# Rows for the FFN turned by the DMA engines as two 16-bit halves, and a new order of steps, in the SSD phase of a hybrid decoder layer

## The chip, the cores and the metric

One NeuronCore of a Trainium2 chip runs the whole layer in one launch. Times are device microseconds of that core. The engines are named as in the profile: PE (TensorE, matrix products and its weight loads PEld), DVE (VectorE), ACT (ScalarE), POOL (GpSimd), and SP (SyncE), whose queue issues nearly all DMAs.

## The reference

A decoder layer on 2048 tokens of 1024 columns, in float32. What matters here is how its two sub-layers meet: the first mixes tokens (an SSD half and an RWKV-7 half, 512 columns each) and projects the result; the second is a gated FFN that reads normalised rows.

```python
mix = jnp.concatenate([y_ssd, y_rwkv], axis=-1).astype(h.dtype) @ w_out[l]
h = h + _rms_norm(mix, post_mix_norm[l])
hn = _rms_norm(h, pre_ffn_norm[l])
u = _causal_dwconv(hn @ ffn_w_up[l], ffn_conv_w[l], ffn_conv_b[l])
...
def _rms_norm(x, g):
    xf = x.astype(jnp.float32)
    y = xf * lax.rsqrt(jnp.mean(xf * xf, axis=-1, keepdims=True) + NORM_EPS)
```

The FFN multiplies `hn` from the left, so PE needs it with the 1024 columns on the partitions: rows have to be turned into columns on the way. This is the place of the change.

## The kernel before

Three phases follow each other and overlap at their ends. Phase R (to about 1000 us) makes the projections and the RWKV half. Phase S (about 1000 to 1440 us) does the SSD half, the output projection and both norms. Phase F is the FFN. Large products are made in float16 with each operand split into a high and a low half. Phase R turns its own input rows by DMA transposes of such halves (lines 399 and 400, 128 rows by 1024 columns each).

Phase S works on sixteen chunks of 128 tokens. Its loop runs steps n = 1 to 15, each written out by the table `S_PLAN`: a word `c.x` calls method `x` of chunk n, `n.` of chunk n+1, `p.` of n-1, `q.` of n-2, and `s.`/`t.` of a pair of chunks in even or odd steps. `Z` is one of four parts of a later chunk's gate product `z` (three per step, four from step 13 on). PE executes in exactly this order. The other engines' and SP's orders are set by a scheduler that simulates times. After the loop, the table `S_TAIL` mixes the last methods with `F`, pieces of phase F's beginning.

The methods: `begin` turns the inputs (`px`) and makes the scores (`psc`); `decay` makes `Dt`, from the rows R of the running sums (`bc` on PE, exponentials on ACT); `off` adds the old state's part (`pf`); `y` multiplies (`py`); `norm` turns the result (`pY`) and splits it into `Y`; `state` updates the state (`pst`); `keys` turns the keys (`pb`); `o` projects in parts (`yr` is the RWKV half, `xi` loads the residual rows). The pair's methods `steps` (`dt`), `sums` and `flip` (`acs`) make the running sums, which go to DRAM (`rows`) and come back as R for each chunk (`n.rows`).

`post`, in two parts, is the end of a chunk: Square of `m` on ACT with a sum over the row (its elementwise output is junk, written into `hT`), reciprocal root on POOL (`pov`, `por`), gain on DVE, residual added on POOL, write of H, a second Square, `pnv` and `pnr`, and the normalised row on DVE, written over `xi`. Then part 0 and part 1 each turn four blocks of 128 columns on PE (tile `ht`), ACT copies them to `hT`, and after part 1 one DMA writes HN, from which phase F reads its operands `hs`.

```python
ps = (bank(f"ht{self.cf}{part}", "yb") if n >= N - 2 else bank(f"ht{self.cf}{part}", "o", 2))
for u in range(4):
    kt = 4 * part + u
    nc.tensor.transpose(ps[:, u, :], self.xin[:, kt * P:(kt + 1) * P], K.ident)
S.activation(self.hT[:, 4 * part:4 * part + 4, :], ps, AF.Copy)
```

Of the kernel before, what the change touches and what calls it, by code (L numbers as in the profile page):

```python
# [7 lines left out]
F32 = mybir.dt.float32  # L8
F16 = mybir.dt.float16
BF16 = mybir.dt.bfloat16  # L10
AF = mybir.ActivationFunctionType
ALU = mybir.AluOpType
# [5 lines left out]
D = 1024  # L18
P = 128
KT = 8  # L20
# [126 lines left out]
class Space:  # L147
# [27 lines left out]
    "Dt", "pp rr ones3 E", "identb mnegb", "Btok", "Xdt", "Xd", "aend dec sgs sgv sgr", "ST0 ST1", "sq", "yt0",  # L175
)
S_RIGHT = (
    "ident_s mhalf_s", "ssm pov por ss pnv pnr", "Y", "yr", "xi", "m", "gpost", "gpre2", "hT", "yt", "wo",
)
F_EARLY = ("us", "s3", "b0", "b1", "b2", "b3")  # L180
F_MID = (
# [8 lines left out]
c.decay.1 m.z.2 m.z.3 t.steps u.z.0 u.z.1 u.z.2 n.rows c.y u.z.3 c.state  # L190
"""
S_PLAN = """
c.begin c.decay.0 Z c.off p.norm c.keys Z c.decay.1 p.o.0.0 Z t.sums s.steps p.o.0.1 t.flip Z n.rows q.post.0 c.y c.state
p.o.1.0 q.post.1 p.o.1.1
"""
S_QUOTA = (3,) * 12 + (4,) * 3
S_TAIL = """
F F p.o.0.0 p.norm F p.o.0.1 p.o.1.0 p.o.1.1 F q.post.0 F q.post.1 F F F F F F p.post.0 F p.post.1
"""
FIRST = """  # L200
w.0 w.1 w.2 w.3 f.d.0 w.4 w.5 l. f.d.1 f.d.2 f.low.0 f.d.3 w.6 f.low.1 f.d.4 f.d.5 w.7 w.8 f.keys f.scan w.9 w.10 f.norm f.d.6 w.11 f.d.7 f.d.8 f.d.9 f.receptance w.12 f.gram.0 w.13 w.14 w.15 w.16 f.gram.1 f.solve.1 w.17 f.d.10 f.conv.0 w.18 w.19 n.load f.chain.0 f.chain.1 f.conv.1 f.chain.2 w.20 f.d.11 f.d.12 f.d.13 w.21 f.conv.2 f.transposed.0 f.conv.3 f.conv.4 f.conv.5 f.transposed.1 f.conv.6 f.chain.3 f.conv.7
# [42 lines left out]
def bcast_row(tc, K, pool, i, name):  # L244
    t = pool.tile([P, D], F32, name=name)
    tc.nc.scalar.dma_start(t, K.rows[i].partition_broadcast(P))
    return t
# [14 lines left out]
def rsqrt_cols(tc, K, pool, ss, n, scale, eps, name, psum=False, bufs=1):  # L262

    nc = tc.nc
    v = pool.tile([P, n], F32, name=name + "v", tag=name + "v", bufs=bufs)
    r = pool.tile([P, n], F32, name=name + "r", tag=name + "r", bufs=bufs)
    (nc.vector if psum else nc.gpsimd).tensor_scalar(out=v, in0=ss, scalar1=scale, scalar2=eps, op0=ALU.mult, op1=ALU.add)  # L267
    nc.gpsimd.tensor_tensor(out=r, in0=v, in1=K.mhalf[:, :n], op=ALU.pow)  # L268
    return r
# [518 lines left out]
def phase_S(tc, K, x, w_z, w_dt, w_o, XN, XC, YR, H, HN, blocks=8):  # L788
    nc = tc.nc
    V, S, G_ = nc.vector, nc.scalar, nc.gpsimd  # L790
    TB = 256
    wk, psp = Space(tc, "s_"), Space(tc, "sp_", space=PSUM)
# [50 lines left out]
    def bank(name, tag, bufs=1):  # L843
        return psp.tile([P, 4, P], F32, name=name, tag=tag, bufs=bufs)
# [81 lines left out]
    class Chunk:  # L926
# [146 lines left out]
        def post(self, part):  # L1073

            m, n = self.m, self.n
            if part == 0:
                ss = wk.tile([P, 1], F32, name="ssm" + self.cf, tag="ssm")
                self.hT = wk.tile([P, KT, P], F32, name="hT" + self.cf, tag="hT")
                jk = self.hT.rearrange("p a b -> p (a b)")[:, 0:D // 2].bitcast(BF16)
                S.activation(jk, m, AF.Square, accum_out=ss)  # L1080
                r = rsqrt_cols(tc, K, wk, ss, 1, 1.0 / D, EPS, "po")
                V.scalar_tensor_tensor(out=m, in0=m, scalar=r[:, 0:1], in1=gpost, op0=ALU.mult, op1=ALU.mult)
                G_.tensor_tensor(out=m, in0=m, in1=self.xin, op=ALU.add)
                K.marks[n] = nc.sync.dma_start(H[n], m)
                ss = wk.tile([P, 1], F32, name="ssh" + self.cf, tag="ss")
                S.activation(jk, m, AF.Square, accum_out=ss)
                r = rsqrt_cols(tc, K, wk, ss, 1, 1.0 / D, EPS, "pn")
                V.scalar_tensor_tensor(
                    out=self.xin, in0=m, scalar=r[:, 0:1], in1=gpre2, op0=ALU.mult, op1=ALU.mult)
            ps = (bank(f"ht{self.cf}{part}", "yb") if n >= N - 2 else bank(f"ht{self.cf}{part}", "o", 2))  # L1090
            for u in range(4):
                kt = 4 * part + u
                nc.tensor.transpose(ps[:, u, :], self.xin[:, kt * P:(kt + 1) * P], K.ident)
            S.activation(self.hT[:, 4 * part:4 * part + 4, :], ps, AF.Copy)
            if part == 1:
                nc.sync.dma_start(HN[n // 8][:, :, P * (n % 8):P * (n % 8) + P], self.hT)


    N = 2 * blocks
# [45 lines left out]
    gpost = bcast_row(tc, K, wk, 1, "gpost")  # L1145
    gpre2 = bcast_row(tc, K, wk, 2, "gpre2")
# [759 lines left out]
```

## Time and profile before

| | |
|---|---|
| median of three runs | 2689.52 us (2687.17 to 2689.76) |
| the profiled execution | 2683.97 us, its span 2681.7 us |
| busy share of PE, DVE, ACT, POOL | 92%, 71%, 45%, 46% |
| mean granted clock of PE | 0.971 |
| bytes moved by DMA | 310.74 MB, 116 GB/s over the span |

The span is the time from the first to the last instruction of the profiled execution. Busy shares are means over all phases; what a stage is worth is read from its own windows. A row of a group gives the summed time, the mean of one instruction in ns, and the idle time of the engine just before, with what ended it.

### The profile page before, as it was taken

How to read it: one execution, taken by the hardware profiler on the slowest of the kernel's cores; microseconds unless marked ns; L12 is line 12 of the kernel's file. 1: busy time of each engine (PE TensorE's matmuls, PEld its weight loads, DVE VectorE, ACT ScalarE, POOL GpSimd, SP SyncE). 2: the span in 40 equal slices, each digit the busy share in tenths (PEclk: the TensorE clock that was granted, in tenths of full speed). 3: DMA queues.
4: the chain of work that ended last, by engine and by line, in shares of the span. 5: the costliest groups of instructions: out<-in, count | busy, mean ns of one | idle time of the engine just before them, and what ended most of it. 6: DMA issues, size and time to landing. Idle time of an engine off the chain costs nothing. (4 is left out here: it accounts for less than half of the span.)

```text
span 2681.7 us, 53948 instructions
## 1 busy us (share of the span) xinstructions
PE 2475.0 (92%) x21340; PEld 1556.0 (58%) x21340; DVE 1909.1 (71%) x3655; ACT 1207.9 (45%) x2467; POOL 1223.6 (46%) x1324
## 2 busy tenths in 40 slices
PE   5889999999999889999997899999999999999998
PEld 4788888888888855555543344444443444444443
DVE  6768777777777665567677868787789836465557
ACT  6445555555565453344444543434354333123132
POOL 2344444444545343234467565656657523222135
PEclk8899999999999989999999999999999999999999
DMA  6323232232223252334455434443435543333252
GB/s 212 73 61 73 53 60 57 65 81 53 57 60 73 89 174 98 107 115 143 128 194 171 156 138 157 134 169 122 159 124 188 183 149 100 103 102 102 87 158 106
DMA packets 309341, 310.74 MB, mean 116 GB/s; under 512 B 168160, under 2 KB 213600, under 8 KB 305760
## 3 DMA queue, kind: packets, MB, share of 16 engines
q1 hardware_dynamic: 307792, 305.72, 37.9%
q8 instruction: 167, 2.74, 0.4%
q10 hardware_dynamic: 1296, 1.58, 0.2%
q14 instruction: 86, 0.70, 0.1%
HBM read 187.85 MB, written 110.99 MB: 111 GB/s over the span
## 5 line engine op out<-in xcount | busy, mean ns | idle before, releaser
L1378 PE MATMUL u<-b,w 128*128 128x512 f16 x3696 | 816.6, 383 | 30.4 <-ACT w L1219 16.1
L1378 PEld LDWEIGHTS <-w 128*128 128x128 f16 x3696 | 363.3, 99 | 480.0 <-issue 29.7
L289 PE MATMUL d<-xt,wr 128*128 128x129 f16 x5376 | 336.9, 224 | 18.1 <-DMA xt<-xh 15.3
L1614 PE MATMUL d<-dw,fa 128*128 128x512 f16 x1512 | 336.4, 381 | 10.6 <-DVE dw L1578 8.4
L289 PEld LDWEIGHTS <-wr 128*128 128x128 f16 x5376 | 322.8, 100 | 32.5 <-ACT wr L252 15.2
L1614 PEld LDWEIGHTS <-fa 128*128 128x128 f16 x1596 | 157.2, 98 | 212.9 <-issue 26.9
L1396 DVE TENSOR_TENSOR C<-u,C 128x512 f32<-128x512 f32 x220 | 150.5, 685 | 163.0 <-PE u L1378 162.6
L289 PE MATMUL c<-xt,wc 128*128 128x131 f16 x3072 | 205.3, 227 | 23.3 <-ACT tr L429 10.4
L289 PEld LDWEIGHTS <-wc 128*128 128x128 f16 x3072 | 189.4, 100 | 39.9 <-issue 31.9
L1627 DVE TENSOR_TENSOR acc<-d,acc 128x512 f32<-128x512 f32 x212 | 140.2, 682 | 51.8 <-PE d L1614 51.2
L576 DVE TENSOR_TENSOR tmp<-atl,xl 128x60 f32<-128x60 f32 (+24 forms) x465 | 139.5, 300 | 44.9 <-DMA atl<-ATd 28.7
L1431 DVE SCALAR_TENSOR_TENSOR p<-C,fpar,p 128x1024 f32<-128x1024 f32 x88 | 126.4, 1437 | 57.0 <-ACT p L1427 53.6
L1224 POOL TENSOR_TENSOR fa<-p,fa 128x512 f16<-128x512 f32 x100 | 133.2, 1350 | 70.8 <-ACT fa L1219 70.8
L1226 DVE SCALAR_TENSOR_TENSOR w<-us,w 128x512 f16<-128x512 f32 x132 | 116.5, 889 | 61.2 <-ACT w L1219 60.2
L452 DVE SCALAR_TENSOR_TENSOR ca<-rc,cw,ca 128x128 f32<-128x128 f32 x384 | 132.3, 389 | 22.8 <-POOL ca L447 22.6
L1219 ACT ACTIVATE fa<-p 128x512 f16<-128x512 f32 x110 | 66.5, 626 | 162.6 <-DVE p L1444 138.8
L579 DVE TENSOR_TENSOR xl<-xl,tmp 128x60 f32<-128x60 f32 (+24 forms) x465 | 124.7, 268 | 11.3
L1437 POOL COPY fcarry<-C 128x2 f32<-128x2 f32 x88 | 36.1, 410 | 182.6 <-DVE C L1396 182.2
L1431 DVE SCALAR_TENSOR_TENSOR a<-C,fpar,a 128x1024 f32<-128x1024 f32 x88 | 114.3, 1299 | 6.4 <-ACT a L1427 4.6
L1219 ACT ACTIVATE w<-us 128x512 f16<-128x512 f32 x132 | 80.0, 622 | 81.0 <-POOL us L1350 61.9
L1392 ACT ACTIVATE C<-u 128x512 f32<-128x512 f32 x88 | 51.8, 589 | 142.7 <-PE u L1378 125.7
L689 POOL TENSOR_TENSOR tS<-S,Pi 64x256 f32<-64x256 f32 x64 | 40.4, 632 | 163.5 <-DVE S L699 161.1
(316 smaller groups left out, 4550.3 us busy)
## 6 DMA issues: line engine op xcount, KB each, us to landing
UW<-w SPq DMA_DIRECT2D x154, 256.0 KB
w<-UW SPq DMA_DIRECT2D x154, 256.0 KB
us<-in_w_u_dram SPq DMA_DIRECT2D x88, 256.0 KB
DW<-dw SPq DMA_DIRECT2D x70, 256.0 KB
dw<-DW SPq DMA_DIRECT2D x56, 256.0 KB
hs<-HN SPq DMA_DIRECT2D x48, 256.0 KB
r<-in_w_d_dram SPq DMA_DIRECT2D x10, 1024.0 KB
xin<-in_x_dram SPq DMA_DIRECT2D x16, 512.0 KB
```

The lines of the kernel that those rows point to most:

```text
L289: nc.tensor.matmul(ps, w[:, a, kt, :], xt[:, b, kt, cols], start=n == 0, stop=n == 3 * KT - 1)
L452: V.scalar_tensor_tensor(out=acc[:, q], in0=raw[:, q, k:k + 128], scalar=cw[:, g + q, k:k + 1], in1=acc[:, q], op0=ALU.mult, op1=ALU.add)
L576: chain.tensor_tensor(out=tmp[:, :m, :n], in0=atl[:, j, j + 1:32].unsqueeze(1).to_broadcast([P, m, n]), in1=xl[:, :m, j:j + 1].to_broadcas ...
L579: chain.tensor_tensor(out=xl[:, :m, j + 1:32], in0=xl[:, :m, j + 1:32], in1=tmp[:, :m, :n], op=ALU.add)
L1219: S.activation(h, src, AF.Copy, **({} if scale is None else {"scale": scale}))
L1224: {"V": V, "G": G_}[engine].tensor_tensor(out=l, in0=src, in1=h, op=ALU.subtract)
L1226: V.scalar_tensor_tensor(out=l, in0=src, scalar=scale, in1=h, op0=ALU.mult, op1=ALU.subtract)
L1378: nc.tensor.matmul(bk[at], self.w[i][:, u, k, :], self.half.b[i][:, k, v, :], start=start and n == 0, stop=n == 11, skip_group_check=True)
L1396: op("V", .61, lambda: V.tensor_tensor(out=part(j, x), in0=bk[at], in1=part(*a), op=ALU.add), (("u", 4 * s + at), (*(c0, c1)[a[0]], a[1])) ...
L1431: V.scalar_tensor_tensor(out=o[j], in0=C[j][:, 2 - d:1026 - d], scalar=cw[:, g, 2 - d:3 - d], in1=o[j], op0=ALU.mult, op1=ALU.add)
L1614: nc.tensor.matmul(bk[s, t], pairs[m].a[i][:, u, t * P:t * P + P], pairs[m].w[n][0][:, v, :], start=new and m == 0 and u == v == 0, stop=m ...
L1627: V.tensor_tensor(out=acc[j][:, t], in0=bk[s, t], in1=acc[j][:, t], op=ALU.add)
```

## The change

The junk of both Squares goes into a new tile `hl` (float16, 128x1024). Each part of `post` now casts its 512 columns to float16 on ACT (`hi`, into `hl`), subtracts on DVE what that holds from the row (`lo`, float16, written over the row's own first bytes in `xi`), has both turned by DMA transposes on SP into the tile `tu` (one buffer), adds the two on POOL into `hT` (now one tile of 128x4x128 for each part), and writes its half of HN. `S_PLAN` and `S_TAIL` get a new order.

```diff
-    "ident_s mhalf_s", "ssm pov por ss pnv pnr", "Y", "yr", "xi", "m", "gpost", "gpre2", "hT", "yt", "wo",
+    "ident_s mhalf_s", "ssm pov por ss pnv pnr", "Y", "yr", "xi", "m", "gpost", "gpre2", "hT", "hl", "tu", "yt", "wo",
 S_PLAN = """
-c.begin c.decay.0 Z c.off p.norm c.keys Z c.decay.1 p.o.0.0 Z t.sums s.steps p.o.0.1 t.flip Z n.rows q.post.0 c.y c.state
-p.o.1.0 q.post.1 p.o.1.1
+c.begin Z c.off c.decay.0 Z p.norm Z Z c.decay.1 p.o.0.0 p.o.0.1 c.keys t.sums q.post.0 s.steps q.post.1 c.y t.flip
+p.o.1.0 c.state p.o.1.1 n.rows
...
-                self.hT = wk.tile([P, KT, P], F32, name="hT" + self.cf, tag="hT")
-                jk = self.hT.rearrange("p a b -> p (a b)")[:, 0:D // 2].bitcast(BF16)
+                self.hl = wk.tile([P, D], F16, name="hl" + self.cf, tag="hl")
+                jk = self.hl.bitcast(BF16)
...
-            ps = (bank(f"ht{self.cf}{part}", "yb") if n >= N - 2 else bank(f"ht{self.cf}{part}", "o", 2))
-            for u in range(4):
-                kt = 4 * part + u
-                nc.tensor.transpose(ps[:, u, :], self.xin[:, kt * P:(kt + 1) * P], K.ident)
-            S.activation(self.hT[:, 4 * part:4 * part + 4, :], ps, AF.Copy)
-            if part == 1:
-                nc.sync.dma_start(HN[n // 8][:, :, P * (n % 8):P * (n % 8) + P], self.hT)
+            cs = slice(512 * part, 512 * part + 512)
+            hi = self.hl[:, cs]
+            S.activation(hi, self.xin[:, cs], AF.Copy)
+            lo = self.xin[:, 512 * part:512 * part + 256].bitcast(F16)
+            V.tensor_tensor(out=lo, in0=self.xin[:, cs], in1=hi, op=ALU.subtract)
+            tu = wk.tile([P, 2, 4, P], F16, name=f"tu{self.cf}{part}", tag="tu")
+            nc.sync.dma_start_transpose(tu[:, 0], hi)
+            nc.sync.dma_start_transpose(tu[:, 1], lo)
+            hT = wk.tile([P, 4, P], F32, name=f"hT{self.cf}{part}", tag="hT")
+            G_.tensor_tensor(out=hT, in0=tu[:, 0], in1=tu[:, 1], op=ALU.add)
+            nc.sync.dma_start(HN[n // 8][:, 4 * part:4 * part + 4, P * (n % 8):P * (n % 8) + P], hT)
```

In the names below, the number behind a name is the chunk (or pair) and part. On PE, in step 9, between the `o` products of chunk 8 there stood before:

```order
L1068 MATMUL o_80_19993<-wo_18037,Y_8_19961 128x512
L916 MATMUL acs_5_20012<-ident_s_18038,nac_5_19798 16x128
L1093 MATMUL ht_70_20058<-ident_s_18038,xi_7_19732 128x128 x4
L1018 MATMUL py_9_20064<-Xdt_9_19918,Dt_9_19919 128x64 x8
L1038 MATMUL pst_9_20086<-Xd_9_19986,Btok_9_19967 128x256 x2
L1068 LDWEIGHTS yr_8_19988
```

and stands now:

```order
L1068 MATMUL o_80_20021<-wo_18043,Y_8_19994 128x512
L973 MATMUL pb_9_20047<-ident_s_18044,xbc_4_19207 128x128 x2
L905 MATMUL acs_5_20052<-da_5_19859,cst_s_17127 128x16
L1018 MATMUL py_9_20090<-Xdt_9_19945,Dt_9_19946 128x64 x8
L916 MATMUL acs_5_20052<-ident_s_18044,nac_5_19860 16x128
L1068 LDWEIGHTS yr_8_20016
```

The transposes of chunk 7's rows (`ht`) are gone, the keys' transposes (`pb`) and the sums come here, the flip of the sums moves behind `py`, and `pst` behind the next `o` products.

SP's queue in the same step before, from the write of chunk 7's rows of H to that of chunk 8:

```order
L1084 DMA H7_90<-m_7_19734 128x1024 [waits DMAHW2_49,Activation_49,Pool_49]
L924 DMA rows_5_20037<-pp_5_20031 16x384 [waits DMAHW3_49,DVE_49]
L979 DMA R_10_20039<-rows_5_20037 3x8x128 [waits DMAHW4_49,DMAHW3_49]
L979 DMA R_11_20297<-rows_5_20037 3x8x128 [waits DMAHW5_49,PE_49]
L1057 DMA yr_9_20200<-YR4_77 128x8x128 [waits DMAHW6_49,PE_49]
L1059 DMA xi_8_19990<-in_x_dram 128x1024 [waits DMAHW7_49,PE_49]
L1096 DMA HN0_81<-hT_7_20042 1024x1x128 [waits DMAHW0_49,Activation_49]
L1084 DMA H8_91<-m_8_19992 128x1024 [waits DMAHW1_49,Activation_49,Pool_49]
```

and now (DMAHW are the semaphores of other DMAs, the rest those of engines):

```order
L1084 DMA H7_90<-m_7_19764 128x1024 [waits Activation_49,Pool_49]
L1096 DMA_TRANSPOSE tu_70_20076<-hl_7_20058 128x4x128 [waits DMAHW7_49,Activation_49]
L1097 DMA_TRANSPOSE tu_70_20076<-xi_7_19762 128x4x128 [waits DMAHW6_49,DVE_49]
L864 DMA xbc_6_20153<-XC6_71 128x2048 [waits PE_49]
L1100 DMA HN0_81<-hT_70_20079 128x4x128 [waits Pool_49]
L1096 DMA_TRANSPOSE tu_71_20084<-hl_7_20058 128x4x128 [waits DMAHW5_49,DMAHW6_49,DMAHW1_49,Activation_49]
L1097 DMA_TRANSPOSE tu_71_20084<-xi_7_19762 128x4x128 [waits DMAHW2_49,DVE_49]
L924 DMA rows_5_20118<-pp_5_20112 16x384 [waits DMAHW3_49,DVE_49]
L1057 DMA yr_9_20231<-YR4_77 128x8x128 [waits DMAHW4_49,PE_49]
L1059 DMA xi_8_20018<-in_x_dram 128x1024 [waits DMAHW2_49]
L979 DMA R_10_20151<-rows_5_20118 3x8x128 [waits DMAHW3_49]
L979 DMA R_11_20412<-rows_5_20118 3x8x128 [waits DMAHW7_49]
```

Part 0's pair of transposes and its write of HN, then part 1's pair, stand ahead of `rows`, `yr`, `xi` and R; part 1's write of HN follows behind R. The load of `xi` waits for a DMA (the transpose that reads `lo` from the same tile) instead of PE.

ACT's queue at the start of step 9, where the first Square of chunk 7 stood behind the first exponentials:

```order
L1071 ACTIVATE m_7_19734<-o_71_19883 128x512
L988 ACTIVATE Dt_9_19919<-bc_90_19933,nac_4_19329 128x128 x4
L1080 ACTIVATE hT_7_20042,ssm_7_20041<-m_7_19734 128x1024
L993 ACTIVATE aend_9_19920<-bc_90_19933 128x4
L1050 ACTIVATE Y_8_19961<-pY_8_19956 128x4x128
```

and now:

```order
L1071 ACTIVATE m_7_19764<-o_71_19910 128x512
L1080 ACTIVATE hl_7_20058,ssm_7_20057<-m_7_19764 128x1024
L988 ACTIVATE Dt_9_19946<-bc_90_19973,nac_4_19385 128x128 x4
L1050 ACTIVATE Y_8_19994<-pY_8_19989 128x4x128
L993 ACTIVATE aend_9_19947<-bc_90_19973 128x4
```

The Square moves ahead of the exponentials, to where `m` has just been copied from PSUM.

More of the change, by code (lines that the diff above doesn't have):

```diff
@@ L197 @@
 S_TAIL = """
-F F p.o.0.0 p.norm F p.o.0.1 p.o.1.0 p.o.1.1 F q.post.0 F q.post.1 F F F F F F p.post.0 F p.post.1
+F F F p.norm F F p.o.0.0 p.o.0.1 q.post.0 F p.o.1.0 F p.o.1.1 F q.post.1 F F p.post.0 F p.post.1 F
 """
```

## The prediction

> **What bounds the kernel now.** I read the page first, for the share of TensorE (PE), then cut out the stage that the change touches, then read the rows of that stage.
>
> ```profile
> PE 2475.0 (92%) x21340; PEld 1556.0 (58%) x21340; DVE 1909.1 (71%) x3655; ACT 1207.9 (45%) x2467; POOL 1223.6 (46%) x1324
> PE   5889999999999889999997899999999999999998
> ```
>
> PE is busy 92% of the span, and the slices show that the gaps are few. The sixteenth to the twenty-first of these slices (67 us each, 1006 to 1408 us) hold the SSD phase. Steps 2 to 15 of its loop begin where PE starts the `px` transposes of a chunk. The windows below are cut at those starts (columns: stretch, length, busy us of PE, PEld, DVE, ACT, POOL, granted clock, DMA share, GB/s); the first four are steps 3, 5, 9 and 11, the next is step 15, and the sum is that of all fourteen. The row after the sum is the tail, from step 15's end to the last of the SSD phase.
>
> ```profile
> 1055.06:1080.05 24.99, 23.60 (x121) 13.49 (x120) 14.46 (x22) 10.21 (x28) 7.70 (x9) 0.93 0.47 160
> ...
> 1102.99:1130.22 27.23, 25.63 (x121) 14.33 (x119) 12.68 (x21) 9.05 (x26) 7.38 (x9) 0.87 0.33 107
> ...
> 1201.32:1223.93 22.61, 21.91 (x120) 12.66 (x119) 12.58 (x21) 9.05 (x26) 7.38 (x9) 1.00 0.39 129
> ...
> 1248.24:1274.96 26.72, 24.31 (x120) 13.63 (x120) 19.85 (x34) 13.53 (x37) 13.65 (x14) 0.94 0.55 188
> ...
> 1348.00:1376.54 28.54, 25.37 (x119) 14.49 (x118) 20.62 (x27) 14.69 (x36) 14.30 (x16) 0.88 0.59 188
> sum 343.74, PE 325.28 PEld 186.20 DVE 225.61 ACT 152.20 POOL 133.11; mean PE 23.23 PEld 13.30 DVE 16.11 ACT 10.87 POOL 9.51
> ...
> 1376.54:1440.00 63.46, 53.47 (x250) 25.08 (x249) 47.45 (x46) 31.78 (x52) 43.58 (x37) 0.95 0.60 199
> ```
>
> PE works 325.28 of 343.74 us, so the loop is bound by PE: what leaves PE shortens it, as long as no other engine or queue takes over. 18.46 us are idle. The 4.3 us by which step 9 and step 5 differ are partly idle time and partly a lower clock (0.87). Where both come from, PE's timeline shows (start, length; in brackets idle time before it and what ended it): five rows of step 9, three of step 5, two of the tail. The group's row is first.
>
> ```profile
> L1093 PE MATMUL ht<-ident_s,xi 128*128 128x128 f32 x128 | 20.9, 288 | 21.2 <-DVE xi L1088 18.7 <-ACT hT L1094 2.3
> ...
> 1214.20 0.27 PE L916 MATMUL acs<-ident_s,nac 128*16 128x128 f32 x1
> 1215.17 0.66 PE L1093 MATMUL ht<-ident_s,xi 128*128 128x128 f32 x4 [0.70 <-DVE xi L1088]
> 1215.66 1.90 PE L1018 MATMUL py<-Xdt,Dt 128*128 128x64 f32 x16
> 1217.39 1.08 PE L1038 MATMUL pst<-Xd,Btok 128*128 128x256 f32 x4
> ...
> 1220.90 0.60 PE L1093 MATMUL ht<-ident_s,xi 128*128 128x128 f32 x4
> 1221.34 1.03 PE L1068 MATMUL o<-wo,Y 128*128 128x512 f16 x4
> ...
> 1118.11 0.66 PE L1093 MATMUL ht<-ident_s,xi 128*128 128x128 f32 x4 [1.52 <-DVE xi L1088]
> 1118.61 2.66 PE L1018 MATMUL py<-Xdt,Dt 128*128 128x64 f32 x16
> 1121.06 2.02 PE L1038 MATMUL pst<-Xd,Btok 128*128 128x256 f32 x4
> ...
> 1403.83 0.66 PE L1093 MATMUL ht<-ident_s,xi 128*128 128x128 f32 x4 [2.28 <-ACT hT L1094]
> 1427.25 1.09 PE L1093 MATMUL ht<-ident_s,xi 128*128 128x128 f32 x4 [7.22 <-DVE xi L1088]
> ```
>
> The first four `ht` transposes stand in PE's queue ahead of `py` and wait for `xi`, the last link of a long chain over ACT, POOL and DVE. After the wait of 1.52 us the same `py` takes 2.66 instead of 1.90 us and `pst` 2.02 instead of 1.08: the clock has fallen.
>
> **What leaves PE.** From start to start, the two groups of four hold PE for 1215.66 - 1215.17 = 0.49 and 1221.34 - 1220.90 = 0.44 us, 0.93 a chunk, 13.0 us in fourteen steps (term A). The group idled 21.2 us; 7.22 and 2.28 belong to the tail, so 11.7 us of waiting leave the loop (term B). The lower clock cost (1 - clock) times the length of the step: 1.7, 3.5, 1.6 and 3.4 us in steps 3, 5, 11 and 15, together 10.3 (term C); in step 5 it follows the `ht` wait directly, and I take the other three for the same. A + B + C = 35.0 us, which leaves 308.7 us or 22.05 a step. The other 6.8 us of idle time I leave as they are.
>
> The rule in the Trainium skill, TensorE: Matmul & The Clock Gate, Rules for kernel authors, is that PE may idle up to about 3 us without losing the clock. By it steps 3, 5 and 11, whose waits are shorter, would owe nothing to `ht`, and C would be 3.4 us, the sum 6.9 us smaller. The trace disagrees: 1.52 us of idle were followed by a step at 0.87.
>
> **What is added, and the new loop.** Each chunk gets two casts on ACT in place of two copies from PSUM, two subtractions on DVE, four transposes and one more write on SP, two additions on POOL. Nearest rows: a cast and a subtraction of 128x512 are `b`, an addition `yt`. The transposes of the RWKV phase show what one of 128x1024 costs SP, and when the write that waits for it goes out; the rest are the links of the chain to `xi`, SP's queue in step 9, and where PE reaches `pY` in it.
>
> ```profile
> L1219 ACT ACTIVATE b<-hs 128x512 f16<-128x512 f32 x48 | 29.5, 626 | 60.2 <-POOL hs L1193 32.2 <-DMA hs<-HN 23.9 <-PE u L1378 4.1
> L1224 DVE TENSOR_TENSOR b<-hs,b 128x512 f16<-128x512 f32 x48 | 48.6, 1026 | 7.7 <-ACT b L1219 7.7
> L1011 POOL TENSOR_TENSOR yt<-yt,of 128x512 f32<-128x512 f32 x16 | 20.8, 1301 | 4.9 <-DVE of L1009 4.9
> ...
> 477.17 1.24 SPq L400 DMA_TRANSPOSE xt<-xin  x1
> ...
> 480.52 1.72 SPq L401 DMA_DIRECT2D XN<-xt  x1
> ...
> L1082 DVE SCALAR_TENSOR_TENSOR m<-m,por,gpost 128x1024 f32<-128x1024 f32 x16 | 34.5, 2155 | 19.0 <-POOL por L268 19.0
> L1083 POOL TENSOR_TENSOR m<-m,xi 128x1024 f32<-128x1024 f32 x16 | 39.4, 2462 | 17.8 <-DVE m L1082 17.8
> L1086 ACT ACTIVATE hT<-m 128x1024 bf16<-128x1024 f32 x16 | 16.9, 1056 | 13.2 <-POOL m L1083 13.2
> L1088 DVE SCALAR_TENSOR_TENSOR xi<-m,pnr,gpre 128x1024 f32<-128x1024 f32 x16 | 22.5, 1409 | 21.3 <-POOL pnr L268 21.3
> 1212.98 0.19 POOL L267 TENSOR_SCALAR pnv<-ssh 128x1 f32<-128x1 f32 x1
> 1213.25 0.54 POOL L268 TENSOR_TENSOR pnr<-pnv,mhalf_s 128x1 f32<-128x1 f32 x1
> 1216.20 0.33 SPq L924 DMA_DIRECT2D rows<-pp  x1
> 1218.09 0.60 SPq L979 DMA_DIRECT2D R<-rows  x2
> ...
> 1222.42 0.56 SPq L1096 DMA_DIRECT2D HN<-hT  x1
> ...
> 1205.00 0.60 PE L1048 MATMUL pY<-ident_s,yt 128*128 128x128 f32 x4
> ```
>
> A transpose of 128x1024 holds SP for 1.24 us and has landed at most 480.52 - 478.41 = 2.1 us later. For half the columns I take 0.62 and again 2.1: the issue can cost from 0.62 to 1.24, the landing from about 1 (half) to beyond 2.1, if other traffic is ahead of it.
>
> The halves of `tu` share one buffer, so part 1's transposes wait for part 0's addition on POOL, and POOL reaches the next chunk's `por` only after part 1's addition. That closes a loop from `por` to the next `por`: two tiny POOL steps 0.81, `m` 2.16, sum 2.46, Square 1.06, two tiny steps 0.81, `xi` 1.41, cast 0.63, subtraction 1.03, issue 0.62, landing 2.1, addition 1.30, write's issue 0.56, two issues 1.24, landing 2.1, addition 1.30: 19.6 us, and with some 14 hand-overs at 0.1 (estimate) 21.0. A step has 21.6 without idle time (22.05 - 6.8/14). The loop is just shorter than the step, by less than the gate product `sz` (DVE, ahead of the subtractions in some steps) takes. Behind a late `por` stand `m`, `of`, `Dt` and `dec` on DVE, then `aend` on ACT, and PE's second `bc` waits for that. The other danger is R: its load stands behind the next `xi` load, which waits until part 1 has landed, and takes from its issue about as long as `rows` (1216.20 to 1218.09, 1.9 us); PE wants R when `px`, `psc`, one `z` product and `pf` are done, a little under 1205.00 - 1201.32 = 3.7 us into a step (the same products and `bc` stand ahead of `pY` there); and `t.flip`, now behind `c.y`, makes R later. I put both at 0.7 us a step, 9.8 us (term D), between 0 (everything fits) and 1.5 and more (the first rivals).
>
> The rest lies under cover. 28 subtractions raise DVE from 225.6 to 254 us of some 319, POOL gets 36 us on top of 133; neither fills a step. Casts for copies are 0.63 for 0.59 us. Square no longer waits for the write of HN but for part 1's first landing, about when `m` arrives. `c.keys`, put behind `p.o.0.1`, still precedes `c.state` by `py` and twelve `o` products, 1.73 + 2.59 us, enough for a copy of half a cast's size; `c.off` ahead of `c.decay.0` only gives R more time. The pair `p.o.0.0`, `p.o.0.1` now follow each other, so Y's second half must be there 2.59 us after the second `bc`; DVE makes it ahead of `xi`.
>
> **Tail.** There `ht` cost 2.28 + 7.22 of waiting, 1.9 of work, and (1 - 0.95) x 63.46 = 3.2 of clock: 14.6 us at most, 0 at least. PE would go on with the FFN's products `u`, whose operands DVE (47.5 of 63.5 us busy) and POOL (43.6) make, and these get 4 and 5 us more to do. I take the half, 7 us (term E).
>
> **Sum.** 13.0 + 11.7 + 10.3 - 9.8 + 7 = 32 us. The profiled execution took 2683.97 us, 2.3 more than its span: 2652. The median of the runs is 5.55 us above that execution, so I predict 2657. What PE does later in the FFN is unchanged, its slices are full, and nothing there gives the time back.
>
> **Rivals.**
> 1. The loop over SP becomes the step, 1.5 us longer than PE's work (issues of 1.24 instead of 0.62, three per loop, are 1.9 us; or each landing 0.75 later). For it: 21.0 against 21.6 is a narrow margin. Against: `m` and the sum overlap other DVE work in their rows, alone they are shorter. 14 x 1.5 = 21 us back: 2678.
> 2. Slower: the transposes land late because each part's pair stands behind a load of 1 MB. Two rows of step 9 show such a load, `xbc`, filling the DMA engines:
>
> ```profile
> 1208.00:1209.00 1.00, 1.00 (x6) 0.49 (x5) 1.00 (x2) 0.82 (x4) 0.00 (x0) 1.00 0.97 410
> 1209.00:1210.00 1.00, 1.00 (x7) 0.43 (x5) 1.00 (x3) 0.00 (x0) 0.91 (x1) 1.00 0.93 393
> ```
>
> At 400 bytes per ns 1 MB is 2.6 us; one such delay at each landing is 5 us a step, 73 us in all, less the 9.8 of D: 2720. It decides from 32 / 14 = 2.3 us a step. Against: `xbc` and `xs` come once in two steps, and the queue has them behind part 0's pair or at the step's start.
> The Trainium skill speaks for this side: VectorE: DVE Perf Modes, The three transpose paths, gives a 128x128 block by DMA 1309 ns and on TensorE 390 ns; by that (an estimate) a pair of 4 blocks each would take 10.5 us and the kernel would end far above 2800. The trace disagrees: eight blocks issued and landed in 3.35 us.
> 3. The SSD phase gains, but the FFN can't start sooner: its operands are made in steps 9 to 15 beside the chunks, and DVE and POOL now have less time and more work there. Then half of the loop's 25 us and the tail's 7 go: 2677.
>
> **How the numbers follow.** Forecast 58% (2640 to 2670), rival 1 20%, rival 2 12%, rival 3 10%. What can be told from no change is 0.2%, 5.4 us, so 2684 to 2695 is "same". Faster: 58, 12 of rival 1 (2678 lies 6 us below that border), 8 of rival 3, is 78%; same 8 + 2 = 10%; slower 12%. The low end is the forecast with D at 0 and E at its full 14.6, 2640, less 2; the high end takes in rivals 1 and 3 with their spread and leaves rival 2 out: 2692.
>
> **What would show it.** Right: no `ht` on PE, steps of 22 to 23 us, the clock at 1.00 in steps 3, 5 and 11, PE waiting in the loop only for `aend` or R and under 1 us at a time, HN's additions on POOL ending shortly before `por`. Wrong: `bc` or `z` on PE with waits of over 1.4 us and a lower clock after them (rival 1 or 2: then SP's queue shows a write of HN waiting for its addition, and that for `tu`), or the first `u` waiting for `w` or `b` as long as the loop became shorter (rival 3).

## The result, and the profile after

The changed kernel takes 2673.70 us in the median of six runs (2666.70 to 2676.04), the kernel before beside it 2688.94 us: a ratio of 0.9941, 95% interval 0.9928 to 0.9954. A second set of runs gave 0.9944 (0.9925 to 0.9964). So it is faster by about 15 us, inside the range, but by a little under half of the 32 us forecast. The profiled execution took 2670.79 us (span 2669.0), 13.2 us less than that of before.

The page's first rows for the changed kernel, as shown of before: PE is as full as it was (92%), with 22.5 us less work.

```profile
PE 2452.5 (92%) x21196; PEld 1542.6 (58%) x21212; DVE 1937.3 (73%) x3687; ACT 1211.1 (45%) x2467; POOL 1265.6 (47%) x1356
PE   5889999999999988999987999999988999999998
```

The loop, cut at the starts of `px` as before: steps 3, 5, 9, 11 and 15, and the sum of steps 2 to 15.

```profile
1058.45:1079.72 21.27, 20.87 (x112) 11.89 (x112) 13.88 (x24) 10.04 (x28) 9.92 (x11) 1.00 0.69 209
...
1102.61:1123.46 20.85, 20.70 (x111) 11.86 (x111) 13.33 (x25) 9.04 (x26) 9.13 (x12) 1.00 0.52 152
...
1191.14:1211.99 20.85, 20.70 (x111) 11.90 (x111) 12.88 (x23) 9.04 (x26) 8.69 (x10) 1.00 0.54 150
...
1235.53:1258.55 23.02, 21.12 (x110) 11.81 (x111) 19.74 (x35) 11.10 (x31) 15.14 (x15) 1.00 0.81 239
...
1330.44:1356.99 26.55, 22.70 (x109) 11.84 (x111) 22.19 (x24) 13.87 (x33) 15.79 (x17) 0.94 0.70 209
sum 321.42, PE 299.37 PEld 170.16 DVE 241.30 ACT 151.85 POOL 169.73; mean PE 21.38 PEld 12.15 DVE 17.24 ACT 10.85 POOL 12.12
```

The loop is 22.3 us shorter (343.74 to 321.42). Step 9 and its like are PE's work and nothing else, 20.85 us at full clock. But with PE busy for 299.37 us, 22.1 us are idle, more than the 18.5 before. Who PE waited for in the loop (us in total, times, longest):

```profile
PE bc L986 <- DMA R<-rows: 8.3, 6, 2.0
PE bc L985 <- ACT aend L993: 6.5, 3, 3.7
PE acs L916 <- DVE nac L906: 2.7, 2, 1.5
PE px L958 <- DVE ST L1041: 2.6, 2, 1.5
PE z L940 <- ACT sz L946: 0.7, 3, 0.2
```

Then part of it is lost again. Three stages, of before and of the changed kernel: steps 2 to 9, steps 10 to 15, and the stretch from the first `u` to the first `d` (called tail from here on; it goes further than the prediction's, to where PE reaches the FFN's second kind of product).

```profile
1032.80:1223.93 191.13, 183.05 (x1069) 105.82 (x1068) 115.58 (x230) 78.68 (x220) 60.14 (x72) 0.97 0.34 112
1223.93:1376.54 152.61, 142.23 (x781) 80.38 (x780) 110.03 (x175) 73.52 (x192) 72.97 (x76) 0.97 0.46 149
1376.54:1506.05 129.51, 108.19 (x489) 48.65 (x488) 100.18 (x95) 60.08 (x96) 90.48 (x75) 0.96 0.50 170
```

```profile
1035.57:1211.99 176.42, 168.46 (x997) 97.32 (x1004) 123.52 (x246) 78.64 (x220) 79.31 (x87) 1.00 0.52 144
1211.99:1356.99 145.00, 130.91 (x727) 72.84 (x732) 117.78 (x184) 73.21 (x189) 90.43 (x87) 0.99 0.61 176
1356.99:1490.89 133.90, 110.11 (x474) 47.97 (x473) 109.39 (x103) 61.78 (x99) 96.35 (x81) 0.91 0.56 177
```

Steps 2 to 9 gained 14.7 us, steps 10 to 15 gained 7.6, and the tail lost 4.4 although PE has the last 16 transposes less to do there. The remaining 5 us lie outside these three stages: step 2 started 2.8 us later, and from the first `d` to the end it took 2.5 us more; in a second profile of the same kernel these were 1.0 and 0.3. Of the 4.4 us that the tail lost, 2.5 are more idle time of PE (21.3 to 23.8) and 1.9 more busy time, at a granted clock of 0.91 instead of 0.96. Who PE waited for in the tail, before and in the changed kernel:

```profile
PE ht L1093 <- DVE xi L1088: 7.2, 1, 7.2
PE u L1378 <- DVE C L1396: 4.4, 5, 1.4
PE u L1378 <- ACT C L1392: 3.9, 1, 3.9
PE u L1378 <- ACT w L1219: 2.5, 1, 2.5
PE ht L1093 <- ACT hT L1094: 2.3, 1, 2.3
```

```profile
PE u L1382 <- ACT C L1396: 14.0, 2, 12.0
PE u L1382 <- DVE b L1228: 4.2, 2, 3.3
PE u L1382 <- DVE C L1400: 3.4, 2, 2.7
PE u L1382 <- DVE w L1230: 2.2, 1, 2.2
```

The 9.5 us of waiting for `ht` are gone. In their place PE waits 17.4 us for `C` (which takes a finished `u` out of PE's bank) instead of 8.3, and 4.2 us for `b`.

### The profile page after: what moved, and what is told of

The parts are those of the page before. It is cut to its first block, busy times and chain, and to the rows that moved or that the text cites. A ratio compares the mean times of both kernels' runs of the same rounds, so it can differ in the third digit from the quotient of the medians.

```text
span 2669.0 us, 53890 instructions
## 1 busy us (share of the span) xinstructions
PE 2452.5 (92%) x21196; PEld 1542.6 (58%) x21212; DVE 1937.3 (73%) x3687; ACT 1211.1 (45%) x2467; POOL 1265.6 (47%) x1356
## 5 line engine op out<-in xcount | busy, mean ns | idle before, releaser
L1354 POOL TENSOR_TENSOR us<-us,us 128x512 f32<-128x512 f32 x66 | 100.4, 1521 | 26.5 <-DVE w L1230 19.9
```

The lines of the kernel that those rows point to most:

```text
L1354: op("G", 1.25, lambda: G_.tensor_tensor(out=st[o], in0=st[a], in1=st[b], op=alu), (n[a], n[b]), (n[o],))
```

## The experiments

All ratios are to the kernel before on the same chip. The stages are from each kernel's own profile, in us. Where a kernel was profiled twice, the stages differed by up to 2, 4 and 2 us, so a difference of 2 or 3 us in one row says nothing alone.

| kernel | ratio (95%) | steps 2-9 | steps 10-15 | tail |
|---|---|---|---|---|
| before | 1 | 191.1 | 152.6 | 129.5 |
| changed | 0.9941 (0.9928-0.9954) | 176.4 | 145.0 | 133.9 |
| changed, again | 0.9944 (0.9925-0.9964) | 174.2 | 145.9 | 135.4 |
| order alone | 0.9963 (0.9948-0.9978) | 182.2 | 140.6 | 137.9 |
| turn alone | 0.9968 (0.9956-0.9980) | 180.5 | 145.0 | 139.2 |
| chunks 14, 15 on PE | 0.9950 (0.9933-0.9967) | 175.7 | 146.8 | 136.6 |
| r late | 0.9915 (0.9899-0.9931) | 174.0 | 148.2 | 128.0 |
| r late, again | 0.9926 (0.9908-0.9945) | 173.5 | 143.9 | 129.9 |
| before, r late | 0.9974 (0.9959-0.9989) | 192.6 | 150.9 | 124.2 |
| order alone, r late | 0.9963 (0.9949-0.9977) | 181.9 | 140.9 | 132.5 |
| r late, `lo` in its own tile | 0.9931 (0.9915-0.9946) | 176.3 | 143.4 | 136.1 |
| r late, two `tu` | 0.9949 (0.9930-0.9968) | 180.4 | 141.6 | 135.3 |
| r late, no subtraction | 0.9969 (0.9957-0.9981) | 183.9 | 145.8 | 129.4 |
| r late, one transpose | 0.9915 (0.9897-0.9933) | 179.1 | 138.6 | 127.5 |
| r late, subtraction on POOL | 0.9928 (0.9910-0.9947) | 174.8 | 144.6 | 129.9 |
| r late, early flip | 0.9949 (0.9934-0.9964) | 179.2 | 152.0 | 128.1 |
| r late, `b` low on ACT | 0.9916 (0.9901-0.9930) | 177.6 | 147.6 | 126.6 |
| r late, `hs` late | 1.0005 (0.9993-1.0016) | 173.0 | 147.9 | 146.0 |
| r late, post early | 0.9939 (0.9926-0.9953) | 178.1 | 146.2 | 131.0 |
| r late, old S_TAIL | 0.9931 (0.9918-0.9945) | 173.4 | 148.9 | 130.8 |

### The change in two parts

The first kernel is the one before with only the two tables replaced; the second is the changed one with the old tables.

```diff
 S_PLAN = """
-c.begin c.decay.0 Z c.off p.norm c.keys Z ...
+c.begin Z c.off c.decay.0 Z p.norm Z Z ...
 S_TAIL = """
-F F p.o.0.0 p.norm F ...
+F F F p.norm F F ...
```

> The kernel before with the new S_PLAN and S_TAIL alone; rows are still turned on PE. Theory (the gain comes from what leaves PE, and the order only makes room for it): the ht waits stay in the loop at 8 to 15 us, the time is 2683 to 2692. Rival (the new order is what shortens the loop): steps 2 to 15 take 330 us or less instead of 343.7, and the time is 2670 to 2680.

> The changed kernel with the old S_PLAN and S_TAIL: rows turned by DMA, steps in the old order. Theory: terms A, B and C come without the order, the loop takes 320 to 328 us and the time is 2668 to 2678. Rival (the new order is needed, without it the transposes come late in SP's queue): the loop takes over 335 us and the time is 2682 or more.

Order alone gives 9.9 us by its ratio, turn alone 8.6, both together 15.8. In the loop they don't add up at all: 322.8 us with the order, 325.4 with the turn, 321.4 with both. My theory for the first was wrong; that for the second (320 to 328 us, 2668 to 2678) held with 325.4 us and 2676.3. The waits of the first in the loop, and its stages:

```profile
PE bc L985 <- ACT aend L993: 4.8, 4, 1.9
PE ht L1093 <- ACT m L1071: 3.6, 3, 1.8
PE z L940 <- ACT sz L946: 0.7, 3, 0.2
```

```profile
1037.87:1220.08 182.21, 177.31 (x1062) 104.27 (x1069) 110.31 (x230) 77.66 (x220) 57.84 (x72) 0.99 0.39 122
1220.08:1360.65 140.57, 134.16 (x775) 77.65 (x780) 103.86 (x175) 75.02 (x192) 74.05 (x75) 1.00 0.49 157
1360.65:1498.54 137.89, 113.11 (x490) 50.35 (x489) 101.68 (x96) 60.41 (x96) 90.04 (x76) 0.91 0.47 159
```

The transposes still stand on PE, and no longer wait for `xi`: in step 5 of this kernel DVE makes `xi` 8.8 us after the step's start (1114.84 against 1106.03), in the kernel before 13.8 us (1116.77 against 1102.99). What the turn by DMA adds to the order is seen by comparing this kernel with the changed one: steps 2 to 9 are 6 to 8 us shorter, steps 10 to 15 are 4.4 to 5.3 us longer, the tail 2.5 to 4 us shorter.

The turn without the new order shows the loop over SP and POOL that the prediction described. From step 3 on, in every step but one, `pov`, the first of `por`'s two rows on POOL, starts within 0.1 us of the end of part 1's addition, 2.6 to 6.4 us into the step; in step 5:

```profile
1103.32 1.16 POOL L1099 TENSOR_TENSOR hT<-tu 128x512 f32<-128x512 f16 x1 [3.77 <-DMA tu<-xi]
1104.56 0.19 POOL L267 TENSOR_SCALAR pov<-ssm 128x1 f32<-128x1 f32 x1
```

PE waits 9.4 us for `aend` in that loop, ten times. With the new order, in steps 2 to 10 of the changed kernel, `por` waits for Square on ACT in every step but step 8, and starts 2.1 us into the step.

### The tail: transposes, and the order on ACT

> The changed kernel, but chunks 14 and 15 (whose rows are turned in the tail) are turned on PE and copied by ACT as before. If the transposes in SP's queue hold up the FFN's first loads there (r, us), the tail gets shorter by more than PE's transposes cost: first u to first d under 130 us instead of 133.9, time 2663 to 2670. If the FFN's operands on DVE and POOL set the tail in any case (rival 3), 2672 to 2676. If the transposes on PE are worth in the tail what term E said, 2679 to 2685.

```diff
+            if n >= N - 2:
+                ps = bank(f"ht{self.cf}{part}", "yb")
+                for u in range(4):
+                    ...
+                    nc.tensor.transpose(ps[:, u, :], self.xin[:, kt * P:(kt + 1) * P], K.ident)
+                S.activation(hT, ps, AF.Copy)
+            else:
```

With chunks 14 and 15 turned on PE the tail is 136.6 us, 1.2 to 2.7 more than in the changed kernel. That is hardly more than two profiles of one kernel differ by, and the intervals of the ratios overlap: the turn in the tail is not worth the 7 us of term E, and no loss was seen from it.

The longest wait in the changed kernel's tail, 12.03 us for `C`, ends on ACT. ACT's rows there:

```profile
1436.23 0.63 ACT L1579 ACTIVATE dw<-r 128x512 f16<-128x512 f32 x1 [2.31 <-DMA r<-in_w_d_dram]
1436.77 0.58 ACT L1396 ACTIVATE C<-u 128x512 f32<-128x512 f32 x1
```

`C` empties PE's bank, and stands behind a cast that waits 2.31 us for the weights `r` (and, before it, behind casts `fa` that wait for DVE and POOL); SP issued the load of `r` at 1431.30, behind the last write of HN. The FFN's planner counted `r` as there from the start. The next kernel makes it count `r` of the first pair 11 us later, which puts `C` first.

```diff
+                if n == 0 and self.i == 0:
+                    op("N", 11., lambda: None, (), tuple(self.names))
```

> The changed kernel; only the planner of the FFN counts the first block of down weights (r of pair 0) as there 11 us later, so that ACT gets the copies C ahead of the casts dw that wait for it. Theory (the tail's 12 us wait for C is a matter of the order on ACT behind a late load r): that wait goes, the time falls by 5 to 10 us to 2664 to 2669. Rival 3 (operands made on DVE and POOL set the start of the FFN): other waits, for w or b, take its place within 20 us, the time stays at 2671 to 2676.

> The same kernel as the one with r late before, beside the three others on one chip, as their reference. Expected ratio 0.990 to 0.993, loop 320 to 324 us, tail 127 to 132 us.

> A control: the kernel before (transposes on PE, old order) with only the planner's count of the first r 11 us later. Theory (the cast that waits for r did harm in the changed kernel because PE got there 15 to 20 us earlier while r could not): here it is worth little, ratio to before 0.9985 to 1.0005. Rival (it is a flaw of the tail whatever the SSD phase does): ratio 0.9965 to 0.9985, as much as the 0.0026 between the changed kernel (0.9941) and the same with r late (0.9915).

> The new order and r late, with the rows still turned on PE as before. Theory (order alone made the loop as short as order and turn together, 322.8 against 321.4 us, so the turn by DMA is worth only what it gives the tail, 0 to 5 us): ratio 0.991 to 0.9945. Rival (the turn is worth 8 us or more by itself): ratio 0.995 to 0.997.

The 12 us wait is gone and the tail is 4.0 to 7.5 us shorter in every pairing of the two profiles each. But the control says that this is not what the change lost: the kernel before gains as much (129.5 to 124.2, ratio 0.9974), and so does the tail of order alone (137.9 to 132.5, though its ratio stays at 0.9963). With r late on both sides the changed kernel's tail is still 4 to 6 us longer than that of before: PE waits there for `w` and `b`, 9.6 and 11.4 us in the two profiles, where the kernel before waits 9.5 us for `ht` and not at all for `w` or `b`. The changed kernel with r late, run twice, has the lowest ratios of the complete kernels, 0.9915 and 0.9926; the intervals still touch that of the changed kernel. The theory for the new order with r late missed, and its rival held: with r late on both sides the turn is worth 10 to 13 us on top of the order (0.9963 against 0.9926 and 0.9915), without it 5 to 6 (0.9963 against 0.9944 and 0.9941, and here the intervals overlap).

> The changed kernel once more, unedited, as the reference for the others. Theory (its tail differs from the kernel with r late by the wait for C alone): ratio 0.993 to 0.9955, loop 318 to 323 us, first u to first d 132 to 136 us with one wait for C of 10 us or more, so that r late is worth 3 to 7 us. Rival (the 12 us wait was chance): the tail is at 128 to 131 us and the ratio at 0.991 to 0.993, as with r late.

The second profile of the changed kernel had the wait for `C` again (11.36 us) and R's waits too (7.8 us): they are the kernel's, not chance.

### What bounds the loop: buffers, subtractions, R

Four suspects, each changed on top of r late.

```diff
-            lo = self.xin[:, 512 * part:512 * part + 256].bitcast(F16)
+            lo = self.lo[:, cs]
...
-            tu = wk.tile([P, 2, 4, P], F16, name=f"tu{self.cf}{part}", tag="tu")
+            tu = wk.tile([P, 2, 4, P], F16, name=f"tu{self.cf}{part}", tag="tu", bufs=2)
...
-            V.tensor_tensor(out=lo, in0=self.xin[:, cs], in1=hi, op=ALU.subtract)
+            G_.tensor_tensor(out=lo, in0=self.xin[:, cs], in1=hi, op=ALU.subtract)
...
-... p.o.0.0 p.o.0.1 c.keys t.sums q.post.0 s.steps q.post.1 c.y t.flip
+... p.o.0.0 p.o.0.1 t.sums c.keys q.post.0 t.flip s.steps q.post.1 c.y
```

> The changed kernel with r late, and the low half lo in a tile of its own instead of in the row's own bytes (xi): the next load of xi then waits for DVE's subtraction only, and the load of R no longer stands behind a transpose through it. Theory (term D is R behind xi): the waits of bc for R go, the even steps fall to about 21.3 us, the loop to 310 to 315 us, ratio 0.987 to 0.989. Rival (something else sets the 23 us of the even steps): the loop stays at 319 to 323 us, ratio 0.990 to 0.993.

> The changed kernel with r late, and two buffers for tu: part 1's transposes no longer wait for part 0's addition on POOL. Theory (the loop over SP and POOL sets the step, rival 1): the loop falls to 308 to 316 us, ratio 0.986 to 0.989. Rival (R and the operands of the FFN set it): 319 to 323 us, ratio 0.990 to 0.993.

> The changed kernel with r late, and the subtractions on POOL instead of DVE, nothing left out. If DVE alone sets the pace from step 10 on: 4 to 8 us faster than with them on DVE, ratio 0.986 to 0.990. If POOL is as full there, or both slow each other: ratio 0.991 to 0.996, steps 10 to 15 at 146 us or more.

> The changed kernel with r late, and in S_PLAN the pair's sums right behind the projection's first half and their flip (t.flip) ahead of s.steps and c.y, instead of behind c.y, so that rows goes out about 2 us earlier and R stands ahead of yr and xi in SP's queue. If R's place is what is left of term D: PE's waits for R (5 us, 3 us in the run before) go, steps 4, 6, 8 and 10 are at 21.3 to 21.7 us, steps 2 to 9 at 170 to 173 us, ratio 0.989 to 0.992. If others take its place (aend, nac): steps 2 to 9 stay at 173 to 176 us, ratio 0.992 to 0.994.

None makes the loop shorter (319.6, 322.0, 319.3 and 331.1 us, against 322.2 and 317.4). The first two are not clean trials, for the scheduler also moved R on SP. In the even steps 4 to 10 R's load goes out 3.4 to 3.9 us after the step's start with two `tu` and 1.7 to 3.1 with `lo` in its own tile, where it went 0.1 to 1.2 us after it with r late alone, and PE waits 10.7 and 5.6 us for R, not less than the 2.8 and 5.3 with r late alone. Nor do two `tu` cut the whole loop over SP and POOL: in steps 11 to 13 `por` still starts right behind an addition, which in step 12 waits 1.64 us for the write of HN that reads the one buffer of `hT`. So what R's place and that loop are worth is not known from these two. The early flip did what it was to do: R is waited for no more. Its waits in the loop:

```profile
PE acs L916 <- DVE nac L906: 8.0, 6, 3.0
PE bc L985 <- ACT aend L993: 7.4, 4, 3.1
PE px L958 <- DVE ST L1041: 5.2, 3, 2.9
```

R's 2.8 and 5.3 us are replaced by more waiting for `nac` (8.0 us, with r late alone 4.0 and 2.7) and for the state (5.2, alone 2.7 and 2.8). Taking one wait off PE in this way was no gain.

The last two leave work out: first the subtractions (the second transpose turns `hi` again), then also the second transpose.

```diff
-            V.tensor_tensor(out=lo, in0=self.xin[:, cs], in1=hi, op=ALU.subtract)
...
-            nc.sync.dma_start_transpose(tu[:, 1], lo)
+            nc.sync.dma_start_transpose(tu[:, 1], hi)
```

```diff
-            nc.sync.dma_start_transpose(tu[:, 1], lo)
...
-            G_.tensor_tensor(out=hT, in0=tu[:, 0], in1=tu[:, 1], op=ALU.add)
+            G_.tensor_tensor(out=hT, in0=tu[:, 0], in1=tu[:, 0], op=ALU.add)
```

> The changed kernel with r late, and the 32 subtractions on DVE left out (the second transpose of each pair turns hi again, so HN holds twice the high half): it prices the subtractions. Theory (from step 10 on DVE, which also makes the FFN's operands there, sets the pace; terms D and E failed on that): steps 2 to 9 stay at 173 to 177 us, steps 10 to 15 fall from 148.2 to 136 to 142, the tail by 2 to 5, the ratio to 0.984 to 0.988. Rival (the transposes on SP and their landings set it): steps 10 to 15 stay above 143 us, ratio 0.989 to 0.993.

> As the run without subtractions, and the second transpose of each pair left out too (POOL adds the first one to itself): what it is faster than that run is the price of 32 transposes on SP and in the DMA engines. Theory: 0 to 4 us less, since SP only waits. Rival (SP and landings): R no longer waits, the loop is 6 us or more shorter than in the run without subtractions.

Both theories on DVE failed here: with 32 instructions less on DVE the kernel is slower, 0.9969, and the loop 329.7 us. The reason shows on SP: without the subtraction the load of `xi` waits for less and moved in between a pair's two transposes, `rows` goes out 0.3 to 1.1 us after the start of the even steps, where it had gone 0.3 to 2.0 us ahead of it with r late alone, and PE waits 12.7 us for R instead of 2.8 or 5.3. With one transpose per part R costs 2.7 us, and the loop is 317.6, 12 us less than in the run without subtractions, as that run's rival had it. The price of the subtraction itself is therefore not known from this pair. The loop without it is 7 to 12 us longer than the two with it (322.2 and 317.4), and the only wait that grew is the one for R.

### Operand work for the FFN

```diff
-                                pace(tc, K, d, 8 + k if 0 in wanted else 12 + k // 2)
+                                pace(tc, K, d, 13)
```

> The changed kernel with r late, but the FFN's first operand loads hs wait for the write of chunk 13's rows of H, so that the operands b0 to b3 are made from step 15 on and not beside steps 10 to 14. Theory (operand work beside the chunks is what lengthens steps 10 to 15, and its end sets the tail): steps 10 to 14 fall from 120 us to 108 to 114, while first u to first d grows by 10 us or more, and the time rises: ratio 0.994 to 1.000. Rival (steps 10 to 15 are long for a reason of their own): they stay at 118 us or more.

The stages came as predicted; the ratio, 1.0005, is just above the 0.994 to 1.000 that I gave. The windows: steps 10 to 14, step 15, tail.

```profile
1200.03:1311.02 110.99, 107.95 (x623) 61.31 (x622) 74.22 (x143) 50.21 (x139) 50.63 (x56) 1.00 0.46 129
1311.02:1347.96 36.94, 21.12 (x111) 11.25 (x109) 31.11 (x33) 19.96 (x45) 27.03 (x27) 0.83 0.75 216
1347.96:1493.98 146.02, 115.89 (x472) 48.56 (x473) 122.75 (x111) 63.61 (x100) 109.13 (x84) 0.87 0.58 184
```

Without the FFN's operands beside them, steps 10 to 14 take 111.0 us, PE busy for 108.0 of them at full clock; with r late alone they took 120.0 and 121.7. PE is idle for 3.0 us there instead of 9.4 and 9.8 (10.2 and 11.0 in the two profiles of the changed kernel). The work is not gone: step 15 (15.8 us of it waiting for the first weights `w`) and the tail take 183.0 us together instead of 154.5 and 153.8. So operand work beside the chunks lengthens these steps, and operand work left for the tail lengthens the tail, as the prediction's rival 3 had it. It is not shown that the changed kernel left more of it: when PE starts its first `u`, ACT has made 20 of the casts `b` and 7 of the casts `w` in the kernel before and in the changed one, and DVE 20 and 19 of the subtractions `b`.

```diff
+                    if hf == 0 and i > 3:
+                        src_, h_, l_ = parts()
+                        S.activation(h_, src_, AF.Copy)
+                        S.activation(l_, src_, AF.Copy)
+                        return
```

> The changed kernel with r late; for the FFN's operands b4 to b6 of the first half, which are made in the tail, the subtraction on DVE is left out and ACT writes a second cast into the low half instead: 12 subtractions, 12 to 15 us, less on DVE, 12 x 0.6 us more on ACT. Theory (operand work on DVE sets the tail): the tail falls from 128 to 130 us to 118 to 125, the time by 4 to 10 us, ratio 0.988 to 0.991. Rival (a chain of latencies sets it, DVE has room): the tail stays within 2 us, ratio 0.991 to 0.9935.

This kernel leaves the subtraction out, so its operands are not the right ones; it only prices DVE's work. DVE has 12 to 13 us less to do in the tail (100.35 instead of 112.6 and 113.8), and the tail is 1.4 to 3.3 us shorter. So DVE's busy time as such is not what sets it.

> The changed kernel with r late and another S_TAIL: the projection of chunk 15 three products u earlier, so that chunk 15's gain m stands on DVE ahead of the taps of the FFN's first block, and its transposes and writes come earlier. If the order on DVE makes PE wait for C: the wait of 4.4 us for C in the second block falls below 2.5 us, first u to first d is 123 to 127 us instead of 128 to 130, ratio 0.989 to 0.9915. If another link of the chain takes its place: 128 to 131 us, ratio 0.9915 to 0.994.

> The changed kernel with r late, with S_TAIL of the kernel before and the new S_PLAN. If the new S_TAIL is part of why the tail lost 4 us: first u to first d 122 to 126 us, ratio 0.988 to 0.991. If it is neutral: 127 to 131 us, ratio 0.991 to 0.994. If it is worth something: over 131 us, ratio over 0.994.

Two more orders of the tail (131.0 and 130.8 us): in the first the wait of 4.4 us for `C` became 3.75, and one of 5.24 came behind it. Neither table gains anything that the runs can tell.

What stays open: which chain holds the tail at 127 to 131 us (135 and 136 in the two kernels with a buffer more). PE works some 109 us in it; every wait that was removed (for `ht`, for `C` behind `r`, for `b`) came back in part as another, for `C`, `b` or `w`, which pass between PE, ACT, DVE and POOL. That operand work from ahead of the tail lengthens it is shown (by `hs` late); a single limit was not found.

## Where the prediction was right, and where it failed

**A, PE's transposes.** Right. PE is busy 311.5 us in the loop with the order alone and 299.4 with the turn, at the same clock: 12.1 us, forecast 13.0.

**B and C, the waits for `ht` and the clock.** Right in size: no `ht`, and the clock is 1.00 in every step but the last. The turn is not the only cause. The order by itself removes most of both (`ht` waits 11.5 to 3.6 us, clock 0.97 to 0.99), and the turn by itself removes the first and brings the clock to 0.98. I costed the new table only where it moved R and the keys, and overlooked that it brings `xi` 5 us earlier.

**D, new stalls.** This term was too small, and its place was wrong. 9.8 us were forecast, 0.7 a step. PE's idle time in the loop came to 22.1 us, and 20.5 in the second profile, against the 16.6 of what was left (6.8) plus D: D measured 15.3 and 13.7. In steps 2 to 9 it was right, or too large: idle time outside `ht` grew from 2.6 us to 8.0 and 5.7, so 5.4 and 3.1 against 5.6 forecast. In steps 10 to 15 it grew from 4.4 to 14.1 and 14.8, so 9.7 and 10.4 against 4.2, with waits for `nac` and `ST`, which I hadn't named. The step of the prediction that failed here is "the rest lies under cover": I took the work on DVE and POOL beside PE for free because neither fills a step, and with the FFN's operands beside it, it was not (`hs` late brings the idle time of steps 10 to 14 down to 3.0 us). The order on R's path was read right, its time was not. In step 8 of the changed kernel, the timeline of SP, then two rows of POOL and one of PE:

```profile
1164.01 1.30 SPq L1096 DMA_TRANSPOSE tu<-hl  x1
1165.41 1.28 SPq L1097 DMA_TRANSPOSE tu<-xi  x1
1166.79 0.52 SPq L924 DMA_DIRECT2D rows<-pp  x1
1167.40 0.55 SPq L1057 DMA_DIRECT2D yr<-YR  x1
1168.57 0.36 SPq L1059 DMA_DIRECT2D xi<-in_x_dram  x1
1168.98 0.61 SPq L979 DMA_DIRECT2D R<-rows  x2
...
1168.71 1.16 POOL L1099 TENSOR_TENSOR hT<-tu 128x512 f32<-128x512 f16 x1 [2.63 <-DMA tu<-xi]
1169.95 0.19 POOL L267 TENSOR_SCALAR pov<-ssm 128x1 f32<-128x1 f32 x1
...
1173.10 0.37 PE L986 MATMUL bc<-R,ones 3*128 3x512 bf16 x1 [2.04 <-DMA R<-rows]
```

`rows` stands behind the pair of transposes, R behind `xi`, and has landed 4.1 us after its issue, where I took 1.9. What R's waits alone are worth is not shown: in the one kernel without them (early flip) other waits took their place.

The loop over SP was read right in form. With the turn in the old order it closes in nearly every step, as rival 1 feared. With the new order it closes in step 8 (the two rows of POOL above: the addition ends at 1169.87, `pov` starts at 1169.95) and, in the same way, in steps 11, 12, 13 and 15. In step 15 `por` starts 3.2 us into the step instead of 2.1 or less, and there stands the wait of 3.7 us for `aend`; whether the loop also lies behind the waits of steps 11 to 13 was not settled. Its disputed link, the issue, is at the upper end of what I allowed (1.24, not 0.62); landing was as taken: 2.0 us from the end of the second issue (1166.69) to POOL's addition (1168.71).

**E, the tail.** This is the step that failed most. I took half of PE's 14.6 us there as gain, 7 us, as if the waiting for `ht` would go and PE would go on; the tail lost 4.4 (5.9 in the second profile). The waiting for `ht`, 9.5 us, did go, but 9.1 us more for `C` and 4.2 for `b` came in its place, and the clock fell from 0.96 to 0.91. Part of it is ACT's order around `r` (4.0 to 7.5 us with r late), but the kernel before has that flaw too; of the 4 to 6 us that remain with r late on both sides the cause stays open. That a loop that ends 20 us sooner hands over fewer of the FFN's operands would explain it, but the counts above speak against it, and PE did start its first `u` 19.6 us sooner, which rival 3 ruled out. Order alone lost 8.4 us there and turn alone 9.6, and neither waited mainly for operands: order alone waits 12.1 us for `ht` and 9.9 for `C`, turn alone 16.7 for `C` and 8.8 once for the load of `yr`. Rival 3 had the sign right, with a chance of 10% and 2677 us, but not what PE then waited for. Rival 1's 2678 lies nearly as close to the 2673.70 measured, so neither number speaks for its mechanism.

**The sum.** In the profiled execution the loop gave 22.3 (forecast 25.2), the tail -4.4 (+7), and the stretches outside them -5.3 (0): 12.6 of 32. In the second profile they are 23.7, -5.9 and -1.4: 16.4. Most of what is missing is E, 11 to 13 us. That the time lies inside the range at all is due to its high end, which took in rivals 1 and 3.

**Rival 2, late landings.** It did not come. The rule that spoke for it (the Trainium skill, VectorE: DVE Perf Modes, The three transpose paths, 1309 ns for a 128x128 block), taken block by block as in the prediction (an estimate, 10.5 us for eight), did not hold here: eight blocks were issued and landed in 1168.71 - 1164.01 = 4.7 us.

## What to carry to other kernels

Try the parts of a change apart before you add up their gains: here a new order and a new path for the data each removed the same wait, and together they gave little more than one. Time won in a stage that PE bounds can be lost in part in the next one, where PE waits for what other engines make (here 4.4 to 5.9 of 22.3 to 23.7 us); read the next stage's busy rows and waits before you credit it with anything. And where a scheduler sets a queue's order, an edit that only removes work can be slower, and one that is meant to remove a wait can leave it, since loads move in front of others: look at the queue first.

## What the runs showed of the hardware

**Transposes on SP.** The groups of the changed kernel's transposes (ns min/median/max): one of 128x512 holds SP as long as one of 128x1024 did before (1.24 us).

```profile
L1096 SPq DMA_TRANSPOSE tu<-hl x32: 1216/1235/2136, 1047.7 to 1423.5; - x32
L1097 SPq DMA_TRANSPOSE tu<-xi x32: 1189/1211/2295, 1049.1 to 1424.7; - x32
```

**The clock after a wait.** Over steps 2 to 9 of the twenty profiles, I set the longest wait of PE in a step beside the step's granted clock. Up to 1.33 us the clock stayed at 1.00 each time. From 1.39 to 2.64 us it fell to 0.87 to 0.94 in 13 of 29 steps and stayed at 1.00 in the other 16; the one of 3.71 us was followed by 0.94. A clock of 0.93 over 25 us is 1.75 us lost, 0.87 over 27 us is 3.5 us, twice as much. So a gap of 1.4 us can cost as much again, and one of 2.6 us can cost nothing. By the rule weighed in the prediction (the Trainium skill, TensorE: Matmul & The Clock Gate, under Why this matters for your kernels: no idle gaps of PE over about 3 us) none of the 29 should have cost anything; 13 did. What decides between the two was not tried.
